# Index scores of a sparse-attention layer: the weighted sum over heads on TensorE, as products with diagonal matrices

## The chip, the cores and the metric

One core of a Trainium2 chip runs the whole program in one launch. The metric is the device time of one execution in microseconds (us); lower is better.

## The reference, cut to what matters

The program is two small transformer stacks run one after the other on 256 tokens of width 1024. The last layer (the "odd" layer) attends only to keys that an index chooses. For each block of 128 queries:

```python
logits = jnp.einsum('bqhd,bsd->bqhs', iqi, ik)                 # 8 index heads of 64, one shared key
score  = jnp.einsum('bqh,bqhs->bqs', iwi, jax.nn.relu(logits)) # weighted sum over the heads
score  = jnp.where(kpos <= qpos, score, -inf)
_, idx = lax.top_k(score, 64)                                  # min(256, 256 // 4) keys a query
# ... attention over the chosen keys alone
```

All is float32. `iwi` is one weight for each query and head.

## The kernel before

Products with the large weight matrices are done as three reduced-precision products: `split` makes a high part of a weight tile on ScalarE (line 267, tile `wh`) and a low part on VectorE (line 268, tile `wl`), and `mm3` issues three matmuls (lines 284 to 286). `wh` and `wl` have four buffers each, of 128x1024, so a new split waits until TensorE has used up an old one.

In `dsa` the queries of the index come first (`o_iq`), then keys and index weights (`o_ki`); their evictions rotate them and transpose them by TensorE (lines 911 to 936, 805 to 810). Then, in the text, come `rows_out`, `together(choose(1), choose(0))`, the values (`o_v`, products in the PSUM tag `m` with 256 columns, evicted at line 1161), the attention queries (`query(0)` and `query(1)`, weights `o_q`, tag `m`, 512 columns, evicted by `rotate`, lines 911 to 921) and four attention groups, which read the choice `sel` as a mask (line 723).

`choose(m)` handles the query block m against `nk` = (m + 1) * 128 keys. It has four steps of two heads. Each step does two float32 products of 64 rows (line 1135) into one PSUM tile of tag `d` (four buffers), one Relu on ScalarE (line 1139) into a tile `pT`, and two multiply-adds on VectorE, which add weight times row block to `sc` (lines 1145 and 1147). Then the causal mask is added (line 1150), and eight rounds of "largest eight" and "replace them" (lines 1154 and 1155) mark 64 keys; lines 1157 and 1158 make the mask `sel`. The two generators `choose(1)` and `choose(0)` take turns.

The text is not the order of issue: a list scheduler orders each engine's instructions when the program is built. It prefers what stands earlier in the text, but an instruction whose inputs it expects later gives way to a later one that is ready. At run time each engine follows that order. Tags share buffers: `g2` has two in this phase (the attention groups use it later), `m` two.

Of the kernel before, what the change touches and what calls it, by code (L numbers as in the profile page):

```python
# [12 lines left out]
AF = mybir.ActivationFunctionType  # L13
ALU = mybir.AluOpType
AX = mybir.AxisListType

P = 128
# [141 lines left out]
def tile_net(ctx: ExitStack, tc: tile.TileContext, a: dict, out: bass.AP):  # L159
    nc = tc.nc  # L160
    V, S, G, PE = nc.vector, nc.scalar, nc.gpsimd, nc.tensor
# [17 lines left out]
    def t_part(tag, n, bufs, dt=F32):  # L179
        return part[0].tile([P, n], dt, tag=tag, name=tag, bufs=bufs)  # L180

    def psd():
        return ps_p.tile([P, 512], F32, tag="d", name="d", bufs=4)
# [7 lines left out]
    def sm(tag, n, bufs=4):  # L191
        return t_keep("s_" + tag, n, bufs)

    def a8(dt=F32):
        return t_keep("a8", 2048, 6, dt)
# [4 lines left out]
    def g2(bufs=None):  # L200
        return t_part("g2", 2 * T, bufs or lay["g2"]).rearrange("p (s t) -> p s t", s=2)
# [13 lines left out]
    ident, a_gain = cst[:, 0:P], cst[:, P:lead_c]  # L215
    rest = cst[:, lead_c:]
    tri, stri, ones, _, m_caus, iota0, iota1 = (rest[:, n * P:(n + 1) * P] for n in range(7))
# [99 lines left out]
    def new_xt():  # L317
        return tuple(a8(F32R).rearrange("p (k t) -> p k t", k=NK) for _ in range(2))
# [56 lines left out]
    def tok_out(xt, src, cols, evac, psx=None, where=None, loaded=(), ready=()):  # L375

        xh, xl = xt
        for c in range(src.shape[0] // 2):
            ps = [(psx or psd)()[:, 0:cols] for _ in range(2)]
            for kh in range(2):  # L380
                u = 2 * c + kh
                w = ready[u] if u < len(ready) else unit(src[u], 4, where, loaded[u] if u < len(loaded) else None)
                for m in range(2):
                    ts = slice(m * P, (m + 1) * P)
                    for k in range(4):
                        kk = 4 * kh + k
                        mm3(ps[m], xh[:, kk, ts], xl[:, kk, ts], *w[k], kk == 0, kk == NK - 1)
            for m in range(2):
                evac(m, c, ps[m])
# [393 lines left out]
    def half(t, hd, idx=None):  # L783
        return t[(hd % 2) * 64:(hd % 2) * 64 + 64, hd // 2 if idx is None else idx, :]
# [118 lines left out]
    def rotate(ps, m, nh, dup=1, parts=False):  # L903


        n = nh * 64
        t1, t2 = (t_part("rt", 512, lay["rt"])[:, 0:n] for _ in range(2))
        o = None if parts else t_part("rt", 512, lay["rt"])[:, 0:n * dup]
        hv = lambda t: t.rearrange("p (h d) -> p h d", h=nh)
        bc = lambda t, lo, hi: t[:, m, lo:hi].unsqueeze(1).to_broadcast([P, nh, hi - lo])  # L910
        V.tensor_tensor(hv(t1), hv(ps), bc(rope["cos"], 0, 64), op=ALU.mult)
        V.tensor_tensor(hv(t2)[:, :, 0:32], hv(ps)[:, :, 32:64], bc(rope["sin"], 0, 32), op=ALU.mult)
        V.tensor_tensor(hv(t2)[:, :, 32:64], hv(ps)[:, :, 0:32], bc(rope["sin"], 32, 64), op=ALU.mult)
        if parts:
            V.tensor_tensor(t1, t1, t2, op=ALU.add)
            o = []
            for h0 in range(0, nh, 4):
                o.append(t_part("s2", 512, 4))
                o4 = o[-1].rearrange("p (h r d) -> p h r d", h=4, r=2)
                S.activation(o4[:, :, 0, :].bitcast(F32R), hv(t1)[:, h0:h0 + 4, :], AF.Copy)  # L920
                V.tensor_tensor(o4[:, :, 1, :], hv(t1)[:, h0:h0 + 4, :], o4[:, :, 0, :], op=ALU.subtract)
        elif dup == 1:
            V.tensor_tensor(o, t1, t2, op=ALU.add)
        else:
            o4 = o.rearrange("p (h r d) -> p h r d", h=nh, r=dup)
            for r in range(dup):
                V.tensor_tensor(o4[:, :, r, :], hv(t1), hv(t2), op=ALU.add)
        return o

    def tr_copy(src, dst, m, scale=1.0):  # L930

        n = src.shape[1] // P
        ps = pst()
        for c in range(n):
            PE.transpose(ps[:, c * P:(c + 1) * P], src[:, c * P:(c + 1) * P], ident)
        S.activation(dst[:, :, m * P:(m + 1) * P], ps[:, 0:n * P].rearrange("p (k t) -> p k t", k=n),
                     AF.Copy, scale=scale)
# [166 lines left out]
    def dsa():  # L1104
        xt = ahead[2]
        ib, kk = a8(), a8(F32R)
        oT = new_xt()
        ikT = ib[:, 0:256].unsqueeze(1)
        iw = ib[:, 256:272].rearrange("p (m d) -> p m d", m=2)
        iqT = ib[:, 512:1536].rearrange("p (k t) -> p k t", k=4)  # L1110
        sel = t_part("sel", 512, 1, F32R).rearrange("p (m t) -> p m t", m=2)
        kh, kl = (kk[:, i * D:(i + 1) * D].rearrange("p (k t) -> p k t", k=4) for i in range(2))
        vv = ib[:, 1536:2048].rearrange("p (m d) -> p m d", m=2)
        def ev_iq(m, c, ps):
            tr_copy(rotate(ps, m, 8), iqT, m)

        tok_out(xt, a["o_iq"], 512, ev_iq)

        def ev_ki(m, c, ps):
            tr_copy(rotate(ps[:, 256:320], m, 1, dup=2), ikT, m)  # L1120
            V.tensor_scalar(iw[:, m, :], ps[:, 320:328], float(8 ** -0.5 * 64 ** -0.5), None, op0=ALU.mult)
            stack(rotate(ps[:, 0:256], m, 4, dup=2), m, kh, kl)

        tok_out(xt, a["o_ki"], 328, ev_ki)

        def choose(m):

            nk = (m + 1) * P
            sc = t_part("sc", T, 2)[:, 0:nk]
            first = True  # L1130
            for h0 in (0, 1, 4, 5):
                ps = psd()
                for i in range(2):
                    hd = h0 + 2 * i
                    PE.matmul(ps[:, i * nk:(i + 1) * nk], half(iqT, hd)[:, m * P:(m + 1) * P],
                              half(ikT, hd, 0)[:, 0:nk], start=True, stop=True)
                yield
                rl = t_part("pT", 512, 4)
                S.activation(rl[:, 0:2 * nk], ps[:, 0:2 * nk], AF.Relu)
                yield  # L1140
                for i in range(2):
                    hd = h0 + 2 * i
                    r1, w1 = rl[:, i * nk:(i + 1) * nk], iw[:, m, hd:hd + 1]
                    if first:
                        V.tensor_scalar(sc, r1, w1, None, op0=ALU.mult)
                    else:
                        V.scalar_tensor_tensor(sc, r1, w1, sc, op0=ALU.mult, op1=ALU.add)
                    first = False
                yield
            V.tensor_tensor(sc[:, m * P:], sc[:, m * P:], m_caus, op=ALU.add)  # L1150
            yield
            for _ in range(8):
                mx = sm("top", 8)
                V.max(mx, sc)
                V.match_replace(sc, mx, sc, -3e38)
                yield
            V.tensor_scalar(sel[:, m, 0:nk], sc, -3e38, NEG, op0=ALU.not_equal, op1=ALU.mult)
            V.tensor_tensor(sel[:, m, m * P:nk], sel[:, m, m * P:nk], m_caus, op=ALU.add)

        def ev_v(m, c, ps):  # L1160
            S.activation(vv[:, m, :], ps, AF.Copy)

        qs = []

        def query(c, ready=()):
            for _ in range(2):
                q = xn_(F32R) if c == 0 else t_part("qs", D, 2, F32R)
                qs.append(q.rearrange("p (k t) -> p k t", k=4))

            def ev_q(m, _, ps):  # L1170
                for o, q in zip(rotate(ps, m, 8, parts=True), qs[2 * c:]):
                    stack(o, m, q, scale=0.125)

            tok_out(xt, a["o_q"][2 * c:2 * c + 2], 512, ev_q, psm, ready=ready)

        def group(g, psx):
            attend(stacked(qs, kh, kl, 0, lambda hd: g), lambda hd, kb: vv[:, kb, g * 64:(g + 1) * 64],
                   None, oT, g, psx,
                   rmask=lambda m: sel[:, m, 0:(m + 1) * P])

        ada_all("o")
        rows_out("o", mod_scale("o", 4, "o_norm_ffn_2"))
        together(choose(1), choose(0))
        tok_out(xt, a["o_v"], 256, ev_v, psm)
        query(0)
        g_m = spread("o", 2)
        ready = [unit(a["o_q"][2 + u], 4) for u in range(READY)]
        for step in ORD:
            if step == "q":
                query(1, ready)  # L1190
            else:
                group(int(step), psd if step in PSD else psm)
        plan()
        out_proj(oT, a["wo3"], g_m)
# [335 lines left out]
```

## Time and profile before

| | |
|---|---|
| median of 3 runs | 1518.72 us (1516.97 to 1523.04) |
| the profiled execution, its own time | 1518.74 us |
| its span in the trace | 1516.9 us |
| TensorE busy, share of the span | 96% |
| VectorE, ScalarE, GpSimd | 80%, 61%, 1% |

Times in the trace are counted from the start of the span. The span is 1.84 us less than the execution's own time.

### The profile page before, as it was taken

How to read it: one execution, taken by the hardware profiler on the slowest of the kernel's cores; microseconds unless marked ns; L12 is line 12 of the kernel's file. 1: busy time of each engine (PE TensorE's matmuls, PEld its weight loads, DVE VectorE, ACT ScalarE, POOL GpSimd, SP SyncE). 2: the span in 40 equal slices, each digit the busy share in tenths (PEclk: the TensorE clock that was granted, in tenths of full speed). 3: DMA queues.
4: the chain of work that ended last, by engine and by line, in shares of the span. 5: the costliest groups of instructions: out<-in, count | busy, mean ns of one | idle time of the engine just before them, and what ended most of it. 6: DMA issues, size and time to landing. Idle time of an engine off the chain costs nothing.

```text
span 1516.9 us, 23337 instructions
## 1 busy us (share of the span) xinstructions
PE 1451.5 (96%) x8918; PEld 1279.9 (84%) x8918; DVE 1218.5 (80%) x2070; ACT 926.8 (61%) x1562; POOL 15.3 (1%) x26
## 2 busy tenths in 40 slices
PE   7999999999999999899899999989899999999996
PEld 6989999899789999778799998778688888888875
DVE  6789887775699877776798875886898888888996
ACT  7766555555575556665644444544687777777764
POOL 0000000000000000000000000000000000000000
PEclk9999999999999999999999999999899999999999
DMA  8668776364387764272498882531499898899893
GB/s 294 241 221 307 247 251 221 128 219 161 121 299 285 240 235 163 76 264 82 161 344 316 334 315 65 182 139 57 166 339 331 324 352 326 295 363 326 301 353 129
DMA packets 55150, 363.07 MB, mean 239 GB/s; under 512 B 6526, under 2 KB 6886, under 8 KB 16630
## 3 DMA queue, kind: packets, MB, share of 16 engines
q1 hardware_dynamic: 55030, 361.50, 66.2%
q8 instruction: 72, 1.18, 0.3%
q14 instruction: 48, 0.39, 0.1%
HBM read 360.37 MB, written 1.10 MB: 238 GB/s over the span
## 4 chain that ended last, share of the span: by engine, by line
PE 83%; DVE 8%; ACT 4%; DMA 2%; issue 1%; POOL 1%; SPq 0%; POOLq 0%; ACTq 0%; DVEq 0%
PE d L284 13%; PE d L285 12%; PE d L286 12%; PE m L285 9%; PE m L286 9%; PE m L284 9%; PE t L286 3%; PE t L285 3%; PE t L284 3%; DVE wl L268 2%; PE d L771 1%; PE t L329 1%; DMA raw<-in_fin_dram 1%; PE t L760 1%; PE t L1305 1%
## 5 line engine op out<-in xcount | busy, mean ns | idle before, releaser
L268 DVE TENSOR_TENSOR wl<-raw,wh 128x1024 fp32r<-128x1024 f32 (+4 forms) x350 | 370.3, 1073 | 65.6 <-ACT wh L267 64.6
L267 ACT ACTIVATE wh<-raw 128x1024 fp32r<-128x1024 f32 (+4 forms) x350 | 320.5, 936 | 99.5 <-PE m L286 31.1
L268 DVE TENSOR_TENSOR wlx<-raw,whx 128x1024 fp32r<-128x1024 f32 (+2 forms) x164 | 182.2, 1113 | 31.1 <-ACT whx L267 30.6
L284 PE MATMUL d<-wh,a 128*128 128x512 f32 (+4 forms) x448 | 167.5, 375 | 5.6 <-ACT a L350 5.0
L267 ACT ACTIVATE whx<-raw 128x1024 fp32r<-128x1024 f32 (+2 forms) x164 | 157.7, 967 | 24.5 <-PE m L285 10.0
L285 PE MATMUL d<-wl,a 128*128 128x512 f32 (+4 forms) x448 | 167.4, 374 | 3.8 <-DVE wl L268 3.8
L286 PE MATMUL d<-wh,a 128*128 128x512 f32 (+4 forms) x448 | 165.8, 371 | 0.1
L284 PE MATMUL m<-a,wh 128*128 128x256 f32 x496 | 140.7, 284 | 0.0
L286 PE MATMUL m<-a,wl 128*128 128x256 f32 x496 | 140.7, 284 | 0.0
L285 PE MATMUL m<-a,wh 128*128 128x256 f32 x496 | 140.5, 283 | 0.0
L506 DVE SCALAR_TENSOR_TENSOR raw<-raw,silu_c 128x1024 f32<-128x1024 f32 x96 | 115.9, 1217 | 3.5 <-DMA raw<-in_o_ada_dram 2.5
L284 PE MATMUL d<-a,th 128*128 128x512 f32 x264 | 107.2, 406 | 1.3 <-ACT th L571 1.0
L285 PE MATMUL d<-a,th 128*128 128x512 f32 x264 | 104.1, 394 | 0.0
L267 ACT ACTIVATE a<-raw 128x1024 fp32r<-128x1024 f32 (+1 forms) x72 | 70.0, 987 | 55.8 <-PE d L286 50.6
L284 PEld LDWEIGHTS d<-wh,a 128*128 128x128 f32 x448 | 85.8, 191 | 20.0 <-ACT a L350 7.6
L285 PEld LDWEIGHTS d<-wl,a 128*128 128x128 f32 x448 | 85.9, 192 | 18.5 <-DVE wl L268 6.9
L268 DVE TENSOR_TENSOR a<-raw,a 128x1024 fp32r<-128x1024 f32 (+1 forms) x72 | 80.9, 1132 | 21.8 <-ACT a L267 21.3
L286 PE MATMUL d<-a,tl 128*128 128x512 f32 x264 | 97.0, 396 | 0.0
L286 PEld LDWEIGHTS d<-wh,a 128*128 128x128 f32 x448 | 85.9, 192 | 13.2 <-DVE a L353 1.8
L284 PEld LDWEIGHTS m<-a,wh 128*128 128x128 f32 x496 | 93.6, 189 | 1.4 <-issue 0.3
L285 PEld LDWEIGHTS m<-a,wh 128*128 128x128 f32 x496 | 93.5, 188 | 1.5 <-issue 0.3
L286 PEld LDWEIGHTS m<-a,wl 128*128 128x128 f32 x496 | 93.5, 188 | 0.4
(386 smaller groups left out, 3622.3 us busy)
## 6 DMA issues: line engine op xcount, KB each, us to landing
raw<-in_fin_dram SPq DMA_DIRECT2D x66, 1024.0 KB, 5.0
raw<-in_fdn_dram SPq DMA_DIRECT2D x33, 1024.0 KB, 5.0
raw<-in_x_dn_dram SPq DMA_DIRECT2D x31, 1024.0 KB, 6.5
raw<-in_x_up_dram SPq DMA_DIRECT2D x27, 1024.0 KB, 5.9
raw<-in_e_ada_dram SPq DMA_DIRECT2D x24, 1024.0 KB, 4.9
raw<-in_o_ada_dram SPq DMA_DIRECT2D x24, 1024.0 KB, 6.7
raw<-in_x_gate_dram SPq DMA_DIRECT2D x24, 1024.0 KB, 6.9
raw<-in_wo_dram SPq DMA_DIRECT2D x16, 1024.0 KB, 5.1
```

Source lines behind the costliest of these rows:

```text
L267: S.activation(hi[:, cs], r[:, cs], AF.Copy)
L268: V.tensor_tensor(lo[:, cs], r[:, cs], hi[:, cs], op=ALU.subtract)
L284: PE.matmul(ps, lh, rh, start=start, stop=False)
L285: PE.matmul(ps, lh, rl, start=False, stop=False)
L286: PE.matmul(ps, ll, rh, start=False, stop=stop)
L329: PE.transpose(ps[:, c * P:(c + 1) * P], src[:, c * P:(c + 1) * P], ident)
L506: V.scalar_tensor_tensor(rr, rr, 1.0, silu_c, op0=ALU.mult, op1=ALU.mult, accum_out=t[:, i:i + 1])
L760: PE.transpose(pt[:, b * P:(b + 1) * P], s2[:, b * P:(b + 1) * P], ident)
L771: PE.matmul(ps[:, i * 64:(i + 1) * 64], pT[:, b * P:(b + 1) * P], vv(hd, kb), start=kb == 0, stop=kb == m)
L1305: PE.matmul(ps[:, c * T:(c + 1) * T], t[:, m, k * P:(k + 1) * P], gr[:, m].rearrange("p i s -> p (i s)"), start=m == 0, stop=m == 1)
```

## The change

The weighted sum moves from VectorE to TensorE. For every four heads ScalarE makes four matrices of 128x128 that hold the heads' weights on the diagonal: the identity times one weight for each row, by a Copy with a column as scale. They stand in one `g2` tile. A product of such a matrix with the Relu tile is weight times row block, and the eight products of a block accumulate in one PSUM tile `total`, which is one of the four buffers of tag `d` and stays taken until the block's scores are read. The mask is added from PSUM, and for block 1 a ScalarE copy brings the unmasked half to `sc`.

```diff
             sc = t_part("sc", T, 2)[:, 0:nk]
-            first = True
+            total = psd()[:, 0:nk]
+            done = 0
             for h0 in (0, 1, 4, 5):
+                if done % 4 == 0:
+                    dg = g2().rearrange("p s (u t) -> p (s u) t", u=2)
+                    for i, hd in enumerate((h0, h0 + 2, h0 + 1, h0 + 3)):
+                        S.activation(dg[:, i, :], ident, AF.Copy, scale=iw[:, m, hd:hd + 1])
+                    yield
                 ps = psd()
...
                 S.activation(rl[:, 0:2 * nk], ps[:, 0:2 * nk], AF.Relu)
                 yield
                 for i in range(2):
-                    hd = h0 + 2 * i
-                    r1, w1 = rl[:, i * nk:(i + 1) * nk], iw[:, m, hd:hd + 1]
-                    if first:
-                        V.tensor_scalar(sc, r1, w1, None, op0=ALU.mult)
-                    else:
-                        V.scalar_tensor_tensor(sc, r1, w1, sc, op0=ALU.mult, op1=ALU.add)
-                    first = False
+                    PE.matmul(total, dg[:, done % 4, :], rl[:, i * nk:(i + 1) * nk], start=done == 0, stop=done == 7)
+                    done += 1
                 yield
-            V.tensor_tensor(sc[:, m * P:], sc[:, m * P:], m_caus, op=ALU.add)
+            if m:
+                S.activation(sc[:, 0:P], total[:, 0:P], AF.Copy)
+            V.tensor_tensor(sc[:, m * P:], total[:, m * P:], m_caus, op=ALU.add)
```

## Rows read from the trace of the kernel before

**Rows 1.** Page, chain that ended last: shares of the span by engine.
```profile
PE 83%; DVE 8%; ACT 4%; DMA 2%; issue 1%; POOL 1%; SPq 0%; POOLq 0%; ACTq 0%; DVEq 0%
```

**Rows 2.** Windows: stretch; length, busy us (instructions) of PE, PEld, DVE, ACT, POOL; clock; DMA.
```profile
975.00:980.00 5.00, 5.00 (x32) 4.36 (x31) 5.00 (x18) 3.05 (x7) 0.00 (x0) 1.00 0.64 233
980.00:985.00 5.00, 3.83 (x17) 2.76 (x15) 5.00 (x27) 2.12 (x2) 0.00 (x0) 1.00 0.80 227
985.00:990.00 5.00, 0.00 (x0) 0.00 (x0) 5.00 (x23) 0.00 (x0) 0.00 (x0) 0.82 0.00 0
990.00:995.00 5.00, 4.96 (x12) 3.90 (x13) 4.12 (x7) 0.00 (x0) 0.00 (x0) 0.50 0.53 177
```

**Rows 3.** Chain that ended last, 970 to 991: start, length, engine, tile, line.
```profile
978.71 0.34 DVE s_top L1154
...
988.85 1.15 DVE wl L268
...
990.04 0.79 PE m L285
```

**Rows 4.** Timeline, TensorE's wait: start, length, instruction [idle before <- released by].
```profile
983.20 0.63 PE L284 MATMUL m<-wh,a 128*128 128x512 f32 x2
...
990.04 0.79 PE L285 MATMUL m<-wl,a 128*128 128x512 f32 x1 [6.21 <-DVE wl L268]
...
994.90 0.48 PE L285 MATMUL m<-wl,a 128*128 128x512 f32 x1
```

**Rows 5.** Timeline, VectorE after the choice.
```profile
978.63 0.42 DVE L1154 MAX8 s_top<-sc 128x8 f32<-128x256 f32 x1
...
988.77 1.22 DVE L268 TENSOR_TENSOR wl<-raw,wh 128x1024 fp32r<-128x1024 f32 x1
989.90 0.28 DVE L1158 TENSOR_TENSOR sel<-sel,cst 128x128 fp32r<-128x128 f32 x1
990.10 3.49 DVE L268 TENSOR_TENSOR wl<-raw,wh 128x1024 fp32r<-128x1024 f32 x3
...
995.13 0.69 DVE L911 TENSOR_TENSOR rt<-m,cos 128x512 f32<-128x512 f32 x1 [0.98 <-PE m L286]
```

**Rows 6.** Timeline, TensorE: the index products, and float32 products of 256 columns (L1061) elsewhere.
```profile
970.18 1.57 PE L1135 MATMUL d<-a 64*128 64x256 f32 x8
...
972.38 3.52 PE L1135 MATMUL d<-a 64*128 64x256 f32 x24
...
975.83 0.39 PE L285 MATMUL m<-wl,a 128*128 128x256 f32 x1
...
690.58 1.99 PE L1061 MATMUL t<-cumT,xn 8*128 8x256 f32 x8
```

**Rows 7.** Groups by form, TensorE, 970 to 976: busy us, mean ns.
```profile
L1135 PE MATMUL d<-a 64*128 64x256 f32 x16 | 4.2, 402 | 0.1
L1135 PE MATMUL d<-a 64*128 64x128 f32 x16 | 2.4, 271 | 0.0
```

**Rows 8.** Timeline, ScalarE: a Copy with a column as scale (L339); Relu; splits.
```profile
10.92 0.62 ACT L339 ACTIVATE mt<-t,cst 128x128 f32<-128x128 f32 x2
11.42 1.16 ACT L350 ACTIVATE a<-mt 128x512 fp32r<-128x512 f32 x2
...
968.42 1.06 ACT L267 ACTIVATE wh<-raw 128x1024 fp32r<-128x1024 f32 x1 [1.71 <-PE m L286]
...
971.35 0.87 ACT L1139 ACTIVATE pT<-d 128x512 f32<-128x512 f32 x2 [1.22 <-PE d L1135]
...
977.80 0.39 ACT L1161 ACTIVATE a<-m 128x256 f32<-128x256 f32 x1 [0.75 <-PE m L286]
```

**Rows 9.** Groups by form: L339 over the span (ACT), L1147 in 968 to 992 (DVE).
```profile
L339 ACT ACTIVATE mt<-t,cst 128x128 f32<-128x128 f32 x8 | 2.7, 362 | 0.2 <-DVE mt L341 0.2
...
L1147 DVE SCALAR_TENSOR_TENSOR sc<-pT,a,sc 128x256 f32<-128x256 f32 x7 | 3.3, 478 | 0.0
...
L1147 DVE SCALAR_TENSOR_TENSOR sc<-pT,a,sc 128x128 f32<-128x128 f32 x7 | 2.4, 344 | 0.0
```

## Prediction, made before the changed kernel was run

> **What bounds the kernel now.** I read the chain that ended last first. TensorE has 83% of it and VectorE 8% [rows 1], so an edit of VectorE's work pays only where VectorE stands on that chain. Next, the windows around the choice. VectorE is full from 975 to 990, and in 985 to 990 TensorE has no instruction at all; its granted clock averages 0.82 there and 0.50 from 990 to 995, that is 1.2 instead of 2.4 GHz [rows 2]. So this is one of the places. The chain says what ends it: VectorE's rounds of "largest eight" from 978.71, then a split of a weight tile, then TensorE [rows 3]. The timeline gives the size. TensorE's last product before the hole is at 983.20 to 983.83, the next one waits 6.21 us for line 268 until 990.04, and twelve products from 990.04 to 994.90 run slow [rows 4]. Eleven steps in 4.86 us are 0.44 us each. At full clock such a product takes 0.23 us (two products in 983.20 to 983.83, of which the last shows its own 0.40 us of length), so the slow clock costs about 11 x 0.21 = 2.3 us. The pot that the change can reach is 6.2 + 2.3 = 8.5 us, 0.56% of the run.
>
> Why TensorE waits: the scheduler puts the choice before the splits of `o_q`, and the choice always has a ready instruction on VectorE. The high part of the next tile had been made at 968.42 [rows 8], its low part came at 988.77, twenty microseconds later, and three more followed at 990.10 [rows 5].
>
> **What VectorE loses.** Two multiplies and 14 multiply-adds go. The 14 are 3.3 + 2.4 us of duration [rows 9], with the two multiplies at the same price 6.5. Neighbouring durations overlap (three splits of 1.22 us take 3.49 [rows 5]), so I take 5.5 us off VectorE. Line 1150 stays, now from PSUM; I keep its price.
>
> **What TensorE gains in work.** 16 float32 products, eight of 256 and eight of 128 columns, 128 rows. The trace shows a float32 product as two records (32 records for 16 products of line 1135). Line 1061 has eight records of 256 columns in 1.99 us, the last 0.37 us of it being one record's length, so 0.23 us a record [rows 6]; half of it, 0.115, is my estimate for 128 columns. 16 x 0.23 + 16 x 0.115 = 5.5 us. From below: 24 records of line 1135, half of each width, start within 975.83 - 972.38 = 3.45 us, 0.144 each, so 32 are 4.6 us. From above: the durations without overlap, 16 x 0.402 + 16 x 0.271 = 10.8 us [rows 7]. I take 5.5, since line 1061 has the same type and width.
>
> **What ScalarE gains.** 16 diagonals and one copy. Two Copies with a column as scale took 0.50 us from the start of the first to that of the next instruction, 0.25 each [rows 8]; singly 0.362 [rows 9]. 16 x 0.25 = 4.0 us, at most 5.8. ScalarE is busy 3.05 and 2.12 of 5 us [rows 2], so the sum fits. The first eight can run before 970.18, because ScalarE idles 1.71 us before 968.42 [rows 8] and the weights come with `o_ki`; I cost them at nothing, at 2 us if not. The second eight stand between Relus: the block's `g2` buffer must come free first. There I charge 0.7 us, what is left of 2 us beside TensorE's 1.15 us of index products and the Relu's wait.
>
> **What the new order does to the choice.** This is the part I weigh most. Before, TensorE ran all the index products ahead (24 records without a break [rows 6]) and only VectorE was slow. Now each step is a loop through two engines: index products, Relu, diagonal products. The two totals hold two of the four `d` buffers, so only one step of each block is in flight. First step: 970.18 to 972.38 as before, then 5.5 / 4 = 1.4 us of diagonal products, 973.8. Each further step: index products 3.45 / 3 = 1.15, diagonal products 1.4, and a wait for the Relu of about 0.5 (at 971.35 it starts 1.17 us after the products began and takes 0.6, so its result is there at 1.8, when 1.15 us of products are issued [rows 8]; 0.65 us at most). That is 3.05, with 0.7 more in the third step: 973.8 + 3 x 3.05 + 0.7 = 983.65. Block 1 is done 0.5 us sooner; with the mask's 0.28 and a hand-over of 0.2 its first "largest eight" starts at 983.7. Before it was 978.63 [rows 5]: **5.0 us later**. From below (no wait, 4.6 us of products): 972.38 + 4 x 1.15 + 3 x 1.15 = 980.4, 1.9 us later. From above (1 us of wait a step, the second diagonals in full at 8 x 0.36): 973.8 + 3 x 3.55 + 2.9 = 987.4, 8.8 us later.
>
> The Trainium skill, "TensorE: Matmul & The Clock Gate" (Part 3, The mechanism), says that matmuls start and end strictly in the order of the program. By it alone every one of the Relu's waits would be a hole and the new work would cost TensorE 5.5 + 4 x 0.5 = 7.5 us, and its ledger below would gain 1.0 us in place of 3.0. No run here shows yet which.
>
> I take them as filled: the `o_v` products stand after the choice in the text, yet 256-column ones are issued at 975.83, straight behind the index products [rows 6], and their last eviction is at 977.80 [rows 8]. The scheduler puts them into what it sees as a hole.
>
> **The two ledgers.** TensorE: 8.5 us of hole and slow clock against 5.5 of new work. If splits are always in time, it gains 3.0 us. VectorE: the choice ends 5.0 us later, about 995.2 in place of 990.2 [rows 5], but VectorE is free before it and can make the low part that waits since 968.42, and a second one as soon as `o_v` has given its `wl` buffer back. Two of the four splits that stood behind the choice, 2.4 us, move ahead. So VectorE leaves this stretch 2.6 us late. What is late next: the rotation of `query(0)`, which started at 995.13 [rows 5]. It reads the two `m` buffers that `query(1)` needs, and could start no sooner than 995.2. So TensorE, which would be through `query(0)` by 995, waits for the rotation's three reads, about 1.3 us, and then for the two splits still missing, which stand behind or between the rotations. That eats 1.5 to 4 of the 3.0 us. I take 2.7: **no change**, 0.3 us gained, which I put at 1519 (the profiled execution took 1518.74, the median is 1518.72; the span is 1.84 less). For this case 1515.5 to 1523.
>
> **The rivals.**
> 1. *TensorE's ledger alone* (0.2). Splits slip between the choice's last rounds, as one did at 988.77 before line 1158 at 989.90 [rows 5], and TensorE never waits: 1518.7 - 3.0 = 1515.7; 1511 if the new work hides as well, which it can only while TensorE idles anyway.
> 2. *The late choice sets the end* (0.2). If `o_v` ends too late to give its buffer back, only one split moves ahead; TensorE runs into the same hole with the same slow clock, at a time 5.0 us later: 1523.7. With the upper bound of 8.8 us it is 1527.5. It is slower by over 0.5% (7.6 us) from when the first "largest eight" starts at about 986.2. Against it: the Relu's waits leave 4 x 0.5 + 0.7 = 2.7 us of holes, and the `o_v` products that followed the index products took from 975.83 to their last eviction at 977.80, 2.0 us [rows 6, 8]; for it: that is close.
> 3. *The saved 5.5 us come through whole* (0.03): the choice starts at once where it did and everything behind is 5.5 us sooner, 1513.2. Against it stands TensorE's part, which the same stretch must take.
> 4. *The order elsewhere changes* (0.07), since the scheduler plans anew: some us either way, half of it beyond 1523 or below 1515.
>
> My forecast has the remaining 0.5. 0.5% is about what a measurement of this kernel can tell from no change, as the three runs lie 0.4% apart. Beyond 0.5% faster (1511.1): 0.03, from rivals 1 and 4. Beyond 0.5% slower (1526.3): a third of rival 2 and part of rival 4, 0.09. Within: 0.88. The range of 8 in 10 goes from 1513 (rival 1 and 3) to 1526 (rival 2 with most of its bound).
>
> **What would show it.** Lines 1145 and 1147 are gone from VectorE; 32 new records of `total` on TensorE take 4.6 to 5.5 us of issue; sixteen ScalarE Copies at 0.25 to 0.36 us. The first "largest eight" is later by 2 to 9 us, not sooner. At least one split of line 268 stands between 973 and 983. TensorE's hole before 990 is smaller or gone, and a new one of 1 to 4 us stands at the rotation of `query(0)` around 995. The attention groups start within 2 us of where they did. I am wrong if the choice starts sooner than before (then TensorE's work was cheaper or overlapped), if the hole stays at 6 us behind it (rival 2), or if the stages from 1020 on change by more than the shift.

## The result, and the profile of the changed kernel

The change makes the kernel slower: 1529.30 us (1526.13 to 1530.58, 4 runs) against 1517.85 us (1515.48 to 1523.04, 4 runs) of the kernel before, ratio 1.0058 with a 95% interval of 1.0038 to 1.0078. That is 8.8 us of loss by the ratio, where no change was forecast.

The profiled execution has a span of 1527.4 us against 1516.9. Of these 10.5 us, 2.7 are there before the first index product (972.9 against 970.2), in code that the change doesn't touch; in the eleven profiles of the experiments, whose code up to there is the same but for the diagonals of one, it starts between 967.7 and 972.2. So times below are counted from each execution's own first index product. By them the last product of `query(1)` comes 46.5 us after it, against 40.1 before, and the end 554.5 us against 546.7: 6.4 us of the loss lie between the index and the end of `query(1)`, 1.4 behind.

The page's busy times, engine, us, share and instructions; VectorE lost 5.4 us of the 1218.5 that it had, TensorE is at 1463.5 in place of 1451.5, and 2.3 of these 12.0 us lie before the first index product, where the code is the same:

```profile
PE 1463.5 (96%) x8950; PEld 1289.0 (84%) x8950; DVE 1213.1 (79%) x2054; ACT 932.1 (61%) x1579; POOL 15.4 (1%) x26
```

The windows of the stretch, columns as in [rows 2]:

```profile
980.00:985.00 5.00, 5.00 (x26) 4.21 (x25) 1.23 (x1) 4.53 (x13) 0.00 (x0) 1.00 0.63 165
985.00:990.00 5.00, 5.00 (x28) 4.31 (x27) 0.35 (x2) 1.15 (x3) 0.00 (x0) 1.00 0.93 347
990.00:995.00 5.00, 5.00 (x23) 4.04 (x23) 5.00 (x26) 2.12 (x2) 0.00 (x0) 1.00 0.04 16
995.00:1000.00 5.00, 3.58 (x16) 2.56 (x14) 5.00 (x28) 2.12 (x2) 0.00 (x0) 1.00 0.00 0
1000.00:1010.00 10.00, 7.63 (x31) 6.40 (x32) 8.82 (x18) 3.51 (x8) 0.00 (x0) 0.66 0.03 4
```

The hole has moved, not gone. From 980 to 990 TensorE is full and VectorE, which was full there in [rows 2], does 1.58 us of work. Then VectorE is full with the eight rounds, TensorE runs dry behind 998, and in 1000 to 1010 its granted clock averages 0.66.

The timeline of TensorE's index products (line 1141) and diagonal products (line 1148):

```profile
972.92 1.57 PE L1141 MATMUL d<-a 64*128 64x256 f32 x8
...
976.69 1.57 PE L1148 MATMUL d<-pT,g 128*128 128x256 f32 x8
978.20 1.57 PE L1141 MATMUL d<-a 64*128 64x256 f32 x8
979.70 0.39 PE L286 MATMUL m<-wh,a 128*128 128x256 f32 x1
...
980.16 1.47 PE L1148 MATMUL d<-pT,g 128*128 128x256 f32 x8
981.56 1.57 PE L1141 MATMUL d<-a 64*128 64x256 f32 x8
983.06 0.50 PE L285 MATMUL m<-wl,a 128*128 128x512 f32 x1
...
984.79 1.47 PE L1148 MATMUL d<-pT,g 128*128 128x256 f32 x8
986.20 1.57 PE L1141 MATMUL d<-a 64*128 64x256 f32 x8
987.70 0.51 PE L286 MATMUL m<-wh,a 128*128 128x512 f32 x1
...
988.27 1.47 PE L1148 MATMUL d<-pT,g 128*128 128x256 f32 x8
989.50 0.48 PE L285 MATMUL m<-wl,a 128*128 128x512 f32 x1
```

Each step now goes index, Relu, diagonal, index, with a few weight products (lines 284 to 286) between; in [rows 6] 24 index records ran in one piece. The first diagonal products come 3.77 us behind the first index products. ScalarE's timeline says why: seven of the first eight diagonals stand before the Relu, and the second eight before the third:

```profile
972.76 2.14 ACT L1136 ACTIVATE g<-cst,a 128x128 f32<-128x128 f32 x7
...
976.06 0.85 ACT L1145 ACTIVATE pT<-d 128x512 f32<-128x512 f32 x2
...
981.35 2.43 ACT L1136 ACTIVATE g<-cst,a 128x128 f32<-128x128 f32 x8
983.69 0.84 ACT L1145 ACTIVATE pT<-d 128x512 f32<-128x512 f32 x2
```

What VectorE does meanwhile, and the group of the "largest eight" (line 1157; counts, durations, first and last start), first the timeline:

```profile
974.01 2.35 DVE L268 TENSOR_TENSOR wl<-raw,wh 128x1024 fp32r<-128x1024 f32 x2
...
981.49 1.23 DVE L268 TENSOR_TENSOR wl<-raw,wh 128x1024 fp32r<-128x1024 f32 x1 [3.96 <-ACT wh L267]
...
989.64 0.49 DVE L1153 TENSOR_TENSOR sc<-d,cst 128x128 f32<-128x128 f32 x2 [6.93 <-ACT sc L1152]
990.05 0.61 DVE L1157 MAX8 s_top<-sc 128x8 f32<-128x256 f32 x2
...
1004.58 1.22 DVE L268 TENSOR_TENSOR wl<-raw,wh 128x1024 fp32r<-128x1024 f32 x1
```

```profile
L1157 DVE MAX8 s_top<-sc x16: 274/346/419, 990.1 to 998.6; 128x8 f32<-128x256 f32 x8, 128x8 f32<-128x128 f32 x8
```

VectorE waits 6.93 us for the scores. The rounds start 990.05 - 972.92 = 17.1 us after the first index product; in [rows 5, 6] it is 978.63 - 970.18 = 8.4. They are **8.7 us later**. Then TensorE's waits, from its timeline:

```profile
998.18 0.40 PE L286 MATMUL m<-wh,a 128*128 128x512 f32 x1
1000.41 0.69 PE L723 MATMUL d<-sel,masks_r 128*128 128x128 f32 x4 [1.83 <-DVE sel L1161]
1001.67 0.47 PE L284 MATMUL m<-wh,a 128*128 128x512 f32 x1 [0.57 <-DVE rt L913]
1003.54 0.76 PE L284 MATMUL m<-wh,a 128*128 128x512 f32 x1 [1.39 <-DVE rt L913]
```

`query(0)` is through at 998.58. Next in TensorE's order stand mask products of group 0, which need the choice (1.83 us), then products of `query(1)`, which need the `m` buffers that the rotation reads (0.57 and 1.39 us). Until 1009.27 `query(1)` gets no further than its fourth product, most of it at the low clock.

### The profile page after: what moved, and what is told of

Its sections match the earlier page's. It is cut to its first block, busy times and chain, and to the rows that moved or that the text cites. A ratio compares the mean times of both kernels' runs of the same rounds, so it can differ in the third digit from the quotient of the medians.

```text
span 1527.4 us, 23398 instructions
## 1 busy us (share of the span) xinstructions
PE 1463.5 (96%) x8950; PEld 1289.0 (84%) x8950; DVE 1213.1 (79%) x2054; ACT 932.1 (61%) x1579; POOL 15.4 (1%) x26
## 4 chain that ended last, share of the span: by engine, by line
PE 82%; DVE 8%; ACT 4%; DMA 3%; issue 1%; POOL 1%; SPq 0%; POOLq 0%; ACTq 0%; DVEq 0%
PE d L284 12%; PE d L285 12%; PE d L286 12%; PE m L284 9%; PE m L285 9%; PE m L286 9%; PE t L286 3%; PE t L284 3%; PE t L285 3%; DVE wl L268 2%; DMA raw<-in_fin_dram 2%; PE d L771 1%; PE t L329 1%; PE t L760 1%; PE t L1308 1%
```

## The experiments

Each was timed in five rounds beside the kernel before. "Start" is the time from the first index product to the first "largest eight", read from the timelines.

| run | what | start, us | time against before (95%) |
|---|---|---|---|
| before | | 8.4 | 1 |
| changed | | 17.1 | 1.0058 (1.0038 to 1.0078) |
| early_diag | all diagonals first | 18.4 | 1.0066 (1.0051 to 1.0081) |
| after_q1d | `query(1)` in tag `d` | 17.1 | 1.0051 (1.0036 to 1.0067) |
| reduced | one-record diagonal products | 13.9 | 1.0025 (1.0013 to 1.0038) |
| pe_work | before, with dead products | 13.4 | 1.0006 (0.9993 to 1.0019) |
| total_t | totals in tag `t` | 12.6 | 1.0004 (0.9994 to 1.0014) |
| after_late0 | changed, rounds behind `query(0)` | 17.1 | 1.0062 (1.0048 to 1.0076) |
| after_late1 | changed, rounds behind `query(1)` | 17.1 | 1.0024 (1.0012 to 1.0036) |
| before_late0 | before, rounds behind `query(0)` | 10.9 | 1.0021 (1.0008 to 1.0033) |
| before_late1 | before, rounds behind `query(1)` | 10.9 | 0.9954 (0.9937 to 0.9971) |
| late1_t | totals in `t`, rounds behind `query(1)` | 12.6 | 1.0001 (0.9991 to 1.0010) |
| pe_work_late1 | dead products, rounds behind `query(1)` | 13.4 | 0.9999 (0.9988 to 1.0009) |

The theory was that the change loses because the choice starts late; the rival, that TensorE is the bound and any work on it costs its length.

**pe_work.** TensorE's part of the change alone, as dead work.

```diff
+                more = pst()[:, 0:nk]
+                for i in range(2):
+                    PE.matmul(more, ident, rl[:, i * nk:(i + 1) * nk], start=i == 0, stop=i == 1)
                 for i in range(2):
                     hd = h0 + 2 * i
```

> The kernel before, with its multiply-adds on VectorE, and on top the 16 float32 products of the change as dead work: identity times the Relu tile, into a PSUM tile of tag t that nobody reads. Late-choice theory (the change loses because the eight rounds of the choice start 8.8 us later, and TensorE's own 5.7 us would have been hidden in the hole of 6.2 us): the choice stays where it was, the hole before 990 shrinks to 0.5 to 2 us, the slow clock behind it is gone, time -2.5 to +1 us against before (1515 to 1519). Work theory (TensorE is the bound, so 5.7 us of products cost 5.7 us wherever they stand): +5 to +6 us, 1523 to 1524.

```profile
L1157 DVE MAX8 s_top<-sc x16: 271/346/419, 985.6 to 994.1; 128x8 f32<-128x256 f32 x8, 128x8 f32<-128x128 f32 x8
L1135 PE MATMUL d<-a x32: 269/374/481, 972.2 to 983.3; 64*128 64x256 f32 x16, 64*128 64x128 f32 x16
```

Measured +0.06%, within the interval nothing: 16 products in TensorE's stretch were free, or nearly so (the last product of `query(1)` comes 1.1 us later than before). As expected, the hole shrinks, to waits of 0.41 and 1.02 us, and the clock stays at 1.00. The rival falls for this order. But the choice did not stay where it was, as I had expected: it starts 5.0 us later (985.6 - 972.2 = 13.4). So 5 us of delay were free as well.

**total_t.** The totals leave tag `d`; index products get its four buffers back.

```diff
-            total = psd()[:, 0:nk]
+            total = pst()[:, 0:nk]
```

> The changed kernel with its two totals in PSUM tag t instead of d, so that index products have four d buffers again and two steps can be in flight. If the one step in flight makes the choice late: the gaps between the steps close, the first round of largest eight comes 2 to 3.5 us sooner than in the changed kernel (about 14 us after the first index product in place of 17), and the time falls by as much, to +3.5 to +6 us against before. If the diagonals on ScalarE or TensorE's products themselves set the pace: sooner by under 1 us, time within 1 us of the changed kernel.

```profile
970.66 1.57 PE L1141 MATMUL d<-a 64*128 64x256 f32 x8
...
972.51 2.78 PE L1148 MATMUL t<-pT,g 128*128 128x256 f32 x16
975.22 2.54 PE L1141 MATMUL d<-a 64*128 64x256 f32 x16
977.92 2.88 PE L1148 MATMUL t<-pT,g 128*128 128x256 f32 x16 [0.15 <-ACT pT L1145]
```

The timeline shows two steps at a time: index products of two steps (the first at 968.47), then diagonal products of two. The loop through ScalarE is walked twice, not four times; the start is 4.5 us sooner than in the changed kernel, 1.0 more than I had allowed, and the loss is gone (1.0004), which I had not expected: +3.5 to +6 us had been written down. The Trainium skill, "Perfetto Trace Analysis" (Optimizing Tensor Performance, Matmuls), says that independent groups of matmuls should rotate through PSUM banks so that the eviction of one overlaps the next. This pair agrees: holding two of four buffers costs 4.5 us of start and 0.54% of time.

**early_diag.** All 16 diagonals ahead of the loop.

```diff
-                if done % 4 == 0:
-                    dg = g2().rearrange("p s (u t) -> p (s u) t", u=2)
...
+            for hh in (0, 4):
+                dgs.append(t_part("s2", 512, 4).rearrange("p (u t) -> p u t", u=4))
+                for i, hd in enumerate((hh, hh + 2, hh + 1, hh + 3)):
+                    S.activation(dgs[-1][:, i, :], ident, AF.Copy, scale=iw[:, m, hd:hd + 1])
```

> The changed kernel with all 16 diagonal matrices made before the first index product, in four buffers of a tag that is free then, so none stands between two Relus. If the second eight diagonals (2.4 us on ScalarE between the second and the third step) make the choice late: the third step shortens by 1.1 us, the first round of largest eight 1 to 2 us sooner than in the changed kernel and the time 1 to 2 us less. If the loop through TensorE and ScalarE itself does, or the longer first batch takes back what the second gives: within 0.7 us of the changed kernel.

```profile
968.04 2.15 ACT L1136 ACTIVATE s<-cst,a 128x128 f32<-128x128 f32 x7
...
971.05 2.73 ACT L1136 ACTIVATE s<-cst,a 128x128 f32<-128x128 f32 x9
973.68 0.85 ACT L1146 ACTIVATE pT<-d 128x512 f32<-128x512 f32 x2
```

No gain: the third step has no diagonals in it any more, but the first Relu waits for all sixteen. They stand ahead of the loop in the text, yet ScalarE reaches them only at 968.04, 0.16 us before the first index product; the start is 1.3 us later than in the changed kernel, which neither expectation had.

**reduced.** Diagonals and Relu tiles in the reduced type.

```diff
-                        S.activation(dg[:, i, :], ident, AF.Copy, scale=iw[:, m, hd:hd + 1])
+                        S.activation(dg[:, i, :].bitcast(F32R), ident, AF.Copy, scale=iw[:, m, hd:hd + 1])
...
-                S.activation(rl[:, 0:2 * nk], ps[:, 0:2 * nk], AF.Relu)
+                S.activation(rl[:, 0:2 * nk].bitcast(F32R), ps[:, 0:2 * nk], AF.Relu)
...
-                    PE.matmul(total, dg[:, done % 4, :], rl[:, i * nk:(i + 1) * nk], start=done == 0, stop=done == 7)
+                    PE.matmul(total, dg[:, done % 4, :].bitcast(F32R), rl[:, i * nk:(i + 1) * nk].bitcast(F32R), start=done == 0, stop=done == 7)
```

> The changed kernel with the diagonal products in the reduced-precision type (one record a product in place of two, scores of lower precision, so the choice of keys can differ). TensorE's part falls from 5.7 to about 1.5 us. Both theories expect a gain: the work theory 4.2 us, whole; the late-choice theory as much as the first round of largest eight comes sooner, 4 x 0.9 = 3.6 us if the products set the pace of the steps, and under 1.5 us if the order planned for TensorE (weight products between the steps) takes their place.

The start is 3.2 us sooner and the time 0.33% less than the changed kernel's, 5 us. It tells the theories apart less than the others, as both allowed a gain.

**The order on VectorE.** Four runs put the eight rounds further back in the text, in the changed kernel and in the one before (there after the last multiply-add); the scheduler then prefers splits and rotations.

```diff
-            yield
+            yield scored
             for _ in range(8):
...
-        together(choose(1), choose(0))
+        picks = [choose(1), choose(0)]
+        left = list(picks)
+        while left:
+            left = [c for c in left if next(c) is not scored]
...
         query(0)
+        together(*picks)
```

In the two others the last line stands behind `query(1, ready)`.

> The changed kernel, scores as they are, but the eight rounds of the choice stand in the text behind query(0), so VectorE's splits and rotations of query(0) go first and the rounds fill in. Late-choice theory (the late rounds stop VectorE's splits and rotations, and TensorE waits for those): TensorE no longer waits at the rotation, the last product of query(1) comes about 41 to 42 us after the first index product in place of 46.5, and the time falls 4 to 6 us against the changed kernel, to +3 to +5 us against before, what is left being the four splits of query(1) behind the rounds. Work theory: it stays at +6 us or more.

> As the last, but the rounds stand behind query(1) too, so VectorE makes every split and rotation before them where it can. Late-choice theory: TensorE waits for nothing in query(0) and query(1); its ledger then stands alone, 8.5 us of hole and slow clock saved against 5.7 of products: the last product of query(1) at 37 to 39 us, time -1 to -3 us against before, unless the attention groups now wait for the choice (then 0 to +2). Work theory: +5.7 us.

> The kernel before, multiply-adds on VectorE, with the rounds of the choice behind query(0) in the text. If the order on VectorE alone made the hole of 6.2 us and the slow clock behind it: the hole before 990 is gone, the last product of query(1) 33 to 37 us after the first index product in place of 40.1, time -3 to -6 us against before. If the rounds then hold the splits of query(1) and the hole only moves: -1 to +2 us.

> The kernel before with the rounds behind query(1) in the text. TensorE without any hole from the index products to the end of query(1): 8.5 us less there, the last product of query(1) at 32 to 34 us. If the attention groups wait no longer for the choice than the hole was, time -5 to -8 us against before; if they wait for the choice, which then ends only 30 us or later, -1 to -4 us.

Behind `query(0)` nothing is gained: the last product of `query(1)` comes at 45.5 us in place of 46.5 in the changed kernel and at 40.3 in place of 40.1 in the other. I had expected 41 to 42 for the first; that failed, because the four splits of `query(1)` still stand behind the rounds (at 1003.30 in after_late0, 994.79 in before_late0), and those are what TensorE needs next. The times missed as well: after_late0 is 9.4 us slower than before where I had +3 to +5. before_late0 is 0.21% (3.2 us) slower where I had -6 to -3 or -1 to +2: the hole has only moved there, with waits of 1.98 and 1.54 us and a clock of 0.50 from 990 to 1000. Behind `query(1)` the hole is gone. The windows of before_late1:

```profile
969.80:980.00 10.20, 10.17 (x63) 8.82 (x64) 9.95 (x25) 5.97 (x13) 0.00 (x0) 1.00 0.37 127
980.00:990.00 10.00, 10.00 (x44) 7.89 (x43) 10.00 (x28) 4.32 (x6) 0.00 (x0) 1.00 0.99 340
990.00:1001.50 11.50, 11.39 (x59) 9.25 (x57) 11.50 (x42) 6.26 (x10) 0.00 (x0) 1.00 0.29 108
1001.50:1010.00 8.50, 6.68 (x35) 5.92 (x34) 7.71 (x20) 5.39 (x11) 0.00 (x0) 0.70 0.06 10
```

TensorE and VectorE are both full at full clock to the end of `query(1)`, which comes at 31.66 us in place of 40.14. The 8.5 us are the hole and the slow clock of [rows 4]. A part comes back behind it: 0.93 and 0.64 us of waits for the rotation and the choice, and a clock of 0.70. What is left is 0.46%, 7 us (4.3 in the profiled execution, one of the slower half of its six runs): this version beats both kernels. The changed kernel in the same order has `query(1)` done at 38.2 us, 6.6 later and within what I had expected, but it is 0.24% (3.6 us) slower than before, where I had -3 to +2: behind `query(1)` it waits 1.67 and 0.64 us for the rotation and the choice, and needs 511.2 us to the end against 506.6 before.

**Both together.** Two runs ask whether the products are free once no hole is left.

> The changed kernel with both repairs: totals in tag t (the choice starts some 5 us sooner) and the rounds behind query(1) in the text. If, with no hole left, TensorE's own products cost their full price: the last product of query(1) at 37 to 38.5 us after the first index product, as in the run with the rounds behind query(1) alone, the attention groups wait less for the choice, time -1 to +1.5 us against before, and still 4.5 to 6.5 us more than the kernel before with the rounds behind query(1). If the late choice was the whole loss and the products are hidden: -5 to -7 us against before, like that kernel.

> The kernel before with the rounds behind query(1) in the text, and the 16 dead float32 products into tag t. The products cost nothing where a hole took them. If that was only because of the hole: now they cost 5 to 6 us over the same order without them, -1 to +1 us against before. If they are hidden anyway (they stand where TensorE waits for Relus): -5 to -7 us.

They are not. In this order the dead products take before_late1 from 0.9954 to 0.9999, 0.45% or 6.8 us (give or take 0.2% by the two intervals), where they took 0.06% in the old order; the last product of `query(1)` moves from 31.7 to 38.5 us, also 6.8. The changed kernel with both repairs stands at 1.0001 and 37.7 us. The window of the dead products shows no hole, and in each 10 us around it, from 970 to 1010, TensorE is busy for 9.8 or more:

```profile
990.00:1000.00 10.00, 10.00 (x49) 8.07 (x48) 10.00 (x31) 5.46 (x8) 0.00 (x0) 1.00 0.62 211
```

**after_q1d.** `query(1)` leaves the `m` buffers that the rotation of `query(0)` holds.

```diff
-            tok_out(xt, a["o_q"][2 * c:2 * c + 2], 512, ev_q, psm, ready=ready)
+            tok_out(xt, a["o_q"][2 * c:2 * c + 2], 512, ev_q, psd if c else psm, ready=ready)
```

> The changed kernel with the products of query(1) in PSUM tag d instead of m, so they need not wait until the rotation of query(0) has read the two m buffers. If the m buffers alone stop TensorE after the late choice: the last product of query(1) at 41 to 43 us in place of 46.5, time +2 to +4 us against before. If VectorE's order as a whole does (the next split stands behind the rounds and the rotations as well, and the mask products of group 0 wait for the choice in TensorE's order): less than 1.5 us gained, +7 to +9 us.

1.0051: taking `query(1)` out of the `m` buffers gains nothing. It does not clear these buffers, though, since TensorE's order then has mask products into `m` where `query(1)` stood, waiting on the same lines:

```profile
995.20 0.41 PE L723 MATMUL d<-sel,masks_r 128*128 128x128 f32 x2 [1.39 <-DVE sel L1161]
996.46 0.30 PE L723 MATMUL m<-sel,masks_r 128*128 128x128 f32 x1 [0.85 <-DVE rt L913]
998.32 0.45 PE L723 MATMUL m<-sel,masks_r 128*128 128x128 f32 x1 [1.56 <-DVE rt L913]
```

## Why the prediction was wrong

- *What bounds the kernel.* Right. before_late1 takes the hole and the slow clock away and gets 8.5 us at the end of `query(1)`; I had read 8.5.
- *VectorE loses 5.5 us.* Right: 5.4 by the page.
- *TensorE gains 5.5 us.* Right: the spacing of the four groups, to the start of the next product, is 1.51, 1.40, 1.41 and 1.23 us, 5.55 in all. Once exposed they cost 6.0 us (late1_t) to 6.8 (pe_work_late1) at the end of `query(1)`.
- *ScalarE gains 4.0 us, the first eight diagonals at nothing.* The first of three wrong terms. Eight take 2.43 us, so 4.9 in all. And the first eight do not stand in ScalarE's idle time before the split, but behind the key's copies at 972.76, before the Relu: one block's weights are read out of PSUM only at 970.96 (line 1121), when that idle time is over. From the first index product to the end of the first diagonal products it is 5.28 us where I had 3.62: 1.7 us, near the 2 that I had named "if not".
- *What the new order does to the choice.* **This is the step that failed**, by its size: I had 5.0 us later, measured are 8.7, close to the upper bound of 8.8. Of the 3.6 us between, 1.7 are the first step's, above. In each further step the index products take 1.50 us to the next product's start (978.20 to 979.70, and so twice more), where I had taken 1.15, a third of the 24 records that ran in one piece: 1.05 in all. In the third step TensorE's diagonal products come 1.73 us behind the index products, where I had 0.5 + 0.7; the 0.7 did not follow from its own terms either (2 - 1.15 - 0.5 is 0.35). And from 989.50 to the first "largest eight" it is 0.55 us where I had almost nothing, because the ScalarE copy of line 1152 (0.28 us), which I had counted only as work, stands on this path. The wait for the Relu in the second and fourth step, 0.46 and 0.57 us, is the 0.5 I had. The cause that I named for the loop, one step in flight because two totals hold two `d` buffers, is shown by total_t: without it the start is 4.5 us sooner and the loss gone. And where the delay is near the 5.0 us of the forecast, 4.2 in total_t and 5.0 in pe_work, the forecast's "no change" is what was measured.
- *Holes filled by other products.* Right in that TensorE is full from 975 to 998; the filling is planned when the program is built, not chosen at run time. The rule of the Trainium skill that I had weighed, "TensorE: Matmul & The Clock Gate" (Part 3, The mechanism), is that matmuls run strictly in the program's order. The place that comes nearest does not test it: at 1000.41 four mask products held TensorE for 1.83 us, but the products of `query(1)` behind them could not start before 1001.5 either, when line 913 has read their `m` buffer.
- *Two splits move ahead.* Right: the second at 974.01 and the one at 981.49 stood behind the choice before.
- *The wait at the rotation, 1.5 to 4 us of TensorE's 3.0.* Too small. With waits of 1.83, 0.57 and 1.39 us, the next split not made before 1004.58, and the low clock until about 1009, the hole and the slow clock were there again, and TensorE's new work came on top: the end of `query(1)` is 8.3 us later than in after_late1, which has the same work and no hole (46.5 against 38.2), and before it was 8.5 (40.1 against 31.7). So nothing of the pot was gained. The starts in the table show it as a bend: with starts of 12.6 and 13.4 us (total_t, pe_work) time stands still within 0.1%, at 13.9 it is 0.25% more (reduced), at 17.1 0.58%. These kernels differ in TensorE's work too (reduced has 3.3 us less of it), so the bend is a sign and not a measured curve; a part of it is the clock that falls again, and I have not split it further.
- *Rivals.* Rival 2 had the price (1527.5 with the upper bound), by luck, but not its condition: not one split too few, since two had moved, but the splits of `query(1)`, the rotation and the mask products behind late rounds. Its hole with the slow clock did come again. Rival 1 did not occur in any run: with the late start repaired the time is that of before, not 3.0 us less.

Open is how the loss divides between the mask products in TensorE's order, the `m` buffers and the splits of `query(1)`; after_q1d does not part them. The 1.4 us behind `query(1)` were not followed. In the five other runs with the rounds in the old place, two of which lose nothing, that stretch is 507.3 to 508.8 us against 508.0 here and 506.6 before, so the 1.4 may be no more than the spread between executions.

## What to carry to other kernels

Work that moves off a busy engine pays nothing if that engine was only in the way by its order: moving the eight rounds behind `query(1)`, with no operation changed, gave 0.46%, and moving the multiply-adds to TensorE could at best fill the hole that this order removes. Before moving a sum into PSUM, count the buffers that the total holds and the engines that one step now passes; a loop of one step in flight made the result 8.7 us late where the work itself took 5.55. Find the slack of what waits for the result (here delays of 4.2 and 5.0 us cost nothing) and see on which side of it the bounds of the new delay lie.

## What the runs showed of the hardware

The Copy with a column as scale on 128x128 elements takes 0.39 us by itself and 0.30 in a row (eight in 2.43 us). TensorE's granted clock fell to 0.50, 1.2 GHz, in the changed kernel's 1003.5 to 1008 although it had not stood still before: five products, 1.17 us of work, lay in 998.6 to 1003.5. In total_t it was busy 8.21 of 10 us in 990 to 1000, with waits of up to 1.03 us, and kept the full clock; in before_late0 it was busy 8.02 of 10 us in 980 to 990, with one wait of 1.98 us, and the clock was 0.50 from 990 to 1000. The changed kernel's windows:

```profile
998.60:1003.50 4.90, 1.17 (x5) 0.71 (x5) 4.90 (x18) 1.78 (x3) 0.00 (x0) 0.91 0.00 0
1003.50:1006.00 2.50, 2.46 (x10) 2.12 (x10) 2.29 (x4) 0.60 (x1) 0.00 (x0) 0.50 0.00 0
1006.00:1008.00 2.00, 2.00 (x9) 1.66 (x9) 1.02 (x3) 1.21 (x3) 0.00 (x0) 0.50 0.00 0
```
